# Pooled branch of a two-layer encoder: its projection made with tokens on partitions, its moving sums moved among the query and key pieces, its products moved to the second block of keys

## The chip, the cores and the metric

One core of one Trainium2 chip. The metric is the time of the device for one launch, in microseconds (us); the kernel takes some 859 of them. A core has five engines with a queue each, worked through in order: TensorE (PE in the profile, its weight loads PEld), VectorE (DVE), ScalarE (ACT), GpSimd (POOL) and SyncE (SP), which here issues most of the DMAs. Operands lie in SBUF, with 128 partitions; products are summed in PSUM.

## The reference, cut to what matters

256 tokens of width 1024, two layers. In each layer the normalised tokens are multiplied by `w_in`, whose columns are cut into the pooled branch's input `u` (1024 columns), queries, keys and values (1536 each) and two gates. What the change touches is the pooled branch: a centred mean over 2, 4, 8 or 16 tokens, minus the token, then one product per group of channels:

```python
ug = u.reshape(B, S, POOL_GROUPS, POOL_GROUP_DIM)          # 4 groups of 256 channels
pooled = jnp.stack([_centred_mean(ug[:, :, gi], w) for gi, w in enumerate((2, 4, 8, 16))], axis=2) - ug
pool_out = jnp.einsum('bsgc,gcd->bsgd', pooled, w_pool).reshape(B, S, POOL_WIDTH) * pool_scale
...
merged = jax.nn.sigmoid(g_pool) * (pool_out @ w_a) + jax.nn.sigmoid(g_attn) * (attn_out @ w_b)
return merged @ w_o
```

All of it is float32; the attention branch (three groups of four heads with a local bias) and the gated MLP with a convolution over three tokens follow beside and behind it.

## The kernel before, in words

**Products in three passes.** TensorE multiplies in fp32r. To keep the accuracy of float32, both operands are cut into a high and a low part, and three products are made: high by high, high by low, low by high. For the weights this is done as they come: SP loads a megabyte (`raw`), ACT casts half of it to the high part (`wh`, L214), DVE subtracts that to get the low part (`wl`, L216). Such a half (128 by 1024) is a *piece*, and the cast and subtraction are its *split*. `Weights` keeps the pieces in the order of use; five split pieces and three raw loads can be in SBUF at once, and `W.get()` splits as far ahead as its `look` (3, in the middle of a layer 4) and the five buffers allow. The buffer of a piece is free when PE has used it up, so in steady state the split of a piece waits for the use of the one five places earlier, and its load for the split of one six places earlier.

**Two shapes of product.** `proj` gives *channels on partitions*: the weights are the stationary operand, 128 columns at a time, and the tokens stream, 512 wide (both parts against `wh`) and 256 wide (the high part against `wl`): eight of each for 128 channels. `by_tokens` gives *tokens on partitions*: the tokens are stationary, and 512 columns of weights stream; a piece is used by 12 matmuls of 512 columns, and four pieces make 512 columns of the result for all 256 tokens, in two PSUM tiles.

**Crossing.** What is needed with channels on partitions, but was made with tokens there, goes through `cross`: two 32 by 32 block transposes of DVE out of PSUM, one write to DRAM issued by SP, and four reads back issued by POOL, each waiting for the write.

**A layer's first half, in PE's order.** Values; the pooled input (`proj`, eight times 128 channels, L577); then six groups of four pieces, made by `by_tokens` and crossed: queries and keys of block 0, of block 1, of block 2; then `w_a` on the pooled output, the gates, `w_b`, `w_o`. Values and pooled input are put in order by a scheduler. From the first block of queries to the first of the last gates the order of PE, ACT and DVE is that of the source: a dictionary `steps` says which work is recorded behind which piece (numbered 0 to 43, block 0's queries being 0 to 3), and `by_tokens` calls `step` behind each.

**The pooled branch.** For each window `w`, from 16 down to 2: two `proj` results are added up out of PSUM into `u` (with 8 tokens of zeros at each side, L613 and L614), the sums are made by doubling (L1004: one addition for window 2, four for window 16), the edges corrected (L1012, L1016), the mean minus the token made (L1018), and cut into parts (ACT L1025, DVE L1026) in `pl2`. All of that is done by the scheduler among the splits. The products with `w_pool` (`pool_out`, 16 matmuls, L577) stand one window at a time ahead of the pieces 4 to 7, the keys of block 0; from each of their two results DVE and ACT make the parts in `po2` (L1042 to L1047).

**Behind it.** `parts` cuts the crossed queries and keys of block 0 into high and low (`highs`, in the memory that held half of `pl2`), behind pieces 11 and 15. Scores of the heads begin behind piece 24, `w_a` reads `po2` from piece 24 on.

Of the kernel before, what the change touches and what calls it, by code (L numbers as in the profile page):

```python
# [17 lines left out]
P = 128  # L18
# [236 lines left out]
def encoder(ctx, tc, x, w_in, w_pool, pool_scale, w_a, w_b, w_o, norm1, norm2, w_up, conv_w,  # L255
# [45 lines left out]
    for l in range(DEPTH):  # L301
        for g in range(NG):
            c0 = C_V + g * 512
            slots = (("m2", 0, 2), ("m2", 1, 2), ("ybig",), ("at2",)) if g == 0 else ()
            for j in range(2):
                tag = "k1" if l == 0 and g == 1 and j == 0 else None
                W.use(rows(w_in[l], j * 512, 4, c0, 512, tag), slots[2 * j : 2 * j + 2])
        if l == 0:
            W.n_scaled = len(W.pieces)
        for c in range(3, -1, -1):  # L310
            W.use(cols(w_in[l], c * 256))
        for n, pairs in enumerate(BLOCKS):
            for base in (C_Q, C_K):
                pool = ([], [])
                if n == 0 and base == C_K:
                    pool = W.add(
                        w_pool[l].rearrange("g (k p) c -> p (g k) c", p=P), (8, 256),
                        [((lambda t, j=j: t[:, 4 * j : 4 * j + 4, :]), (4, 256)) for j in range(2)],
                    )
                    pool = (pool[:1], pool[1:])  # L320
                for j in range(2):
                    W.use(pool[j] + pairs_of_heads(l, j * 512, base, pairs))
        for w, c0 in ((w_a[l], 0), (w_in[l], C_GP)):
            for c in (c0, c0 + 512):
                W.use(rows(w, 0, 4, c, 512) + rows(w, 512, 4, c, 512))
        for c in (0, 512):
            W.use(rows(w_in[l], 0, 4, C_GA + c, 512) + rows(w_in[l], 512, 4, C_GA + c, 512))
            W.use(rows(w_b[l], 0, 4, c, 512))
        for c in range(4):
            W.use(rows(w_o[l], c * 256))  # L330
        first_up.append((len(W.pieces), len(W.loads)))
        slots = (("v1",), ("ybig",), ("at2",))
        for j in range(2):
            tag = None if j else "k1"
            W.use(rows(w_up[l], j * 512, 4, 0, 512, tag), slots[2 * j : 2 * j + 2])
        for j in range(2):
            W.use(rows(w_up[l], j * 512, 4, DFF, 512))
        halves_done = {}
        for kind, n in PLAN:
            if kind in "AG":  # L340
                j = halves_done.get((kind, n), 0)
                halves_done[kind, n] = j + 1
                W.use(rows(w_up[l], j * 512, 4, (kind == "G") * DFF + n * 512, 512))
            elif kind == "P":
                a = cols(w_up[l], n * P)
                if n >= 4 * NQ:
                    g = cols(w_up[l], DFF + n * P)
                    a = [a[0], g[0], a[1], g[1]]
                W.use(a)
            elif kind == "D":  # L350
                W.use(rows(w_down[l], n * P))
        n_down = sum(2 for kind, _ in PLAN if kind == "D")
        for f in range(n_down, NF, 2):
            W.use(rows(w_down[l], f * P))
# [386 lines left out]
    def cross(rows, y, z, name, after=None):  # L741
# [12 lines left out]
        for q in range(4):  # L754
# [2 lines left out]
                in_=d[:, q].rearrange("(a i) x -> i a x", i=32),  # L757
            )

    def two_parts(tag, name):  # L760


        return big.tile([P, KD, 2, 2, P], F32R, tag=tag, name=name)
# [174 lines left out]
    for l in range(DEPTH):  # L938
# [46 lines left out]
            big.tile([P, KD // 2, 2, 2, P], F32R, tag=tag, name="pl2") for tag in ("ybig", "xn")  # L985
        ]
        pooled = {}
        for gi in range(3, -1, -1):
            w = WINDOWS[gi]
            u = sm.tile([P, 2, S + 2 * PAD], F32, tag="u", name="u")  # L990
            nc.vector.memset(u[:, :, 0:PAD], 0.0)
            nc.vector.memset(u[:, :, PAD + S :], 0.0)
            for j in range(2):
                if l == 0 and (gi, j) == (1, 0):

                    with tc.issue_after(W.last_load.ins):
                        next(bias)
                add_up(in_order(u[:, j, PAD : PAD + S]), [halves(a) for a in proj(x2, 1 + (l > 0))])
            cur, n = u, S + 2 * PAD
            sh = 1  # L1000
            while sh < w:
                nxt = sm.tile([P, 2, S + 2 * PAD], F32, tag="us", name="us")
                n -= sh
                nc.vector.tensor_add(  # L1004
                    out=nxt[:, :, 0:n], in0=cur[:, :, 0:n], in1=cur[:, :, sh : sh + n]
                )
                cur = nxt
                sh *= 2
            hw = w // 2
            o = PAD - hw  # L1010
            e = edge[:, gi, 0:hw].unsqueeze(1).to_broadcast([P, 2, hw])
            nc.vector.tensor_mul(out=cur[:, :, o : o + hw], in0=cur[:, :, o : o + hw], in1=e)  # L1012
            if hw > 1:
                e = edge[:, gi, hw : w - 1].unsqueeze(1).to_broadcast([P, 2, hw - 1])
                r = slice(o + S - hw + 1, o + S)
                nc.vector.tensor_mul(out=cur[:, :, r], in0=cur[:, :, r], in1=e)  # L1016
            pd = sm.tile([P, 2, S], F32, tag="us", name="pd")
            nc.vector.scalar_tensor_tensor(  # L1018
                out=pd, in0=cur[:, :, o : o + S], scalar=1.0 / w, in1=u[:, :, PAD : PAD + S],
                op0=ALU.mult, op1=ALU.subtract,  # L1020
            )
            both = pl2[gi // 2][:, gi % 2 * 2 : gi % 2 * 2 + 2]
            ph, pl = both[:, :, 0], both[:, :, 1]
            pd = pd.rearrange("p k (m t) -> p k t m", t=2)
            nc.scalar.copy(out=ph, in_=pd)  # L1025
            nc.vector.tensor_sub(out=pl, in0=pd, in1=ph.bitcast(F32))  # L1026
            pooled[gi] = both
        def pool_out(po2):
            for j in range(2):
                i, (wh, wl) = W.get()  # L1030
                for gg in range(2):
                    for oc in range(2):
                        ps = acc.tile([P, 2, S], F32, tag="acc", name="pool_ps")
                        cc = slice(oc * P, (oc + 1) * P)
                        two_sums(
                            pooled[2 * j + gg], 2,
                            (ps, lambda k: wh[:, 2 * gg + k, cc], lambda k: wl[:, 2 * gg + k, cc]),
                        )
                        c = 4 * j + 2 * gg + oc
                        sc = hps[:, l, c : c + 1]  # L1040
                        po = sm.tile([P, 2, P], F32, tag="u", name="po")
                        nc.scalar.mul(out=po, in_=halves(ps[:, 1]), mul=sc)  # L1042
                        nc.vector.scalar_tensor_tensor(
                            out=po, in0=halves(ps[:, 0]), scalar=sc, in1=po, op0=ALU.mult, op1=ALU.add
                        )
                        nc.scalar.copy(out=po2[:, c, 0], in_=po)
                        nc.vector.tensor_sub(out=po2[:, c, 1], in0=po, in1=po2[:, c, 0].bitcast(F32))  # L1047
                    if gg:
                        W.free(i)
                    yield  # L1050

        q = big.tile([P, 2, 4, 2, P], F32, tag="q1", name="q")
        kk = big.tile([P, 2, 2 * 4, 4, 32], F32, tag="k1", name="k")
        probs, turned, ptiles = {}, {}, {}

# [73 lines left out]
        def parts(which):  # L1131

            hi = (qh, kh)[which]
            for half in range(2):
                a = kk[:, 1 - which, :, 2 * half : 2 * half + 2].rearrange("p a c j -> p c a j")
                h_, l_ = (
                    b.rearrange("p c t (a j) -> p c (t a) j", j=32)
                    for b in (hi[:, 2 * half : 2 * half + 2], lows[half][:, which])
# [3 lines left out]

        def bring(half):

            a = tmp[:, 0].rearrange("p (a c j) -> p c a j", a=8, c=4)
            nc.scalar.copy(out=q[:, half].rearrange("p c t (a j) -> p c (t a) j", j=32), in_=a)

# [2 lines left out]
        def keep_pa(n):  # L1150
# [4 lines left out]


        steps = {
            11: ((parts, 0),),
            15: ((parts, 1),),
            19: ((bring, 0),),  # L1160
            24: ((scores, 0), (start_turn, 0)),
            26: ((scores, 1), (start_turn, 1)),
# [20 lines left out]
        in_order_of_source = ExitStack()  # L1183
        in_order_of_source.enter_context(tc.manual_schedule(engines={PE, ACT, DVE}))
        W.look = W.LOOK + 1
        tmp = big.tile([P, 2, 1024], F32, tag="at2", name="qk_rows")
        po2 = None
        for n in range(6):
            block, which = divmod(n, 2)
            if n == 1:  # L1190
                po2 = two_parts("m2", "po2")
            ps = by_tokens(x2, 4, then=step, ahead=pool_out(po2) if n == 1 else None)
            y = tmp[:, 1].rearrange("p (t q c j) -> p t q c j", t=2, q=4, c=4)
            if n in (2, 4):
                z = tmp[:, 0].rearrange("p (a c j) -> p a c j", a=8, c=4)
            else:

                z = kk[:, (1, 0, None, 0, None, 1)[n]]
            cross(ps, y, z, "crossing")
            if n == 1:  # L1200

                highs = big.tile([P, 2, HPG, 2, P], F32R, tag="xn", name="highs")
                qh, kh = highs[:, 0], highs[:, 1]
# [97 lines left out]
        def to_z(ps, z, after):  # L1301
            y = big.tile([P, 2, 4, 4, 32], F32, tag="v0", name="crossing")
            cross(ps, y, z, "crossing", after)

        def of_chunk(z, i):
            return z[:, :, i].rearrange("p (t a) j -> p t a j", t=2)

        def by_halves(z):
            ps = by_tokens(x2, 4, end=2)
# [128 lines left out]
```

## Time and profile before

| | us |
|---|---|
| median of three runs | 859.02 (858.85 to 859.89) |
| profiled execution, its own time | 857.63 |
| its span, first to last instruction | 855.8 |
| granted clock of TensorE, mean | 0.997 |
| PE, PEld, DVE, ACT, POOL busy | 847.2, 710.9, 664.3, 490.5, 125.5 |
| DMA | 243 GB/s mean, 207.76 MB |

The times of instructions below come from the profiled execution; 1.8 us of its time lie outside its span. A matmul row's length contains the way through the array, so that the lengths overlap: 512 columns last 0.39 us in a row, but the next begins 0.227 us after. What PE's work takes is therefore read from the chain of work that ended last, in order of time, where every piece runs to the start of the next.

### The profile page before, as it was taken

To read this page: it belongs to the slowest core of one execution; us is meant where nothing else is said; L and a number is where in the kernel's file an instruction comes from. 1 tells how busy PE (TensorE), PEld (TensorE's weight loads), DVE (VectorE), ACT (ScalarE), POOL (GpSimd) and SP (SyncE) were. 2 spreads that over 40 slices of the span, in tenths; PEclk is the share of its full clock that TensorE was granted. 3 is DMA by queue.
4 is the path that set the end of the run, shared out by engine and by line. 5 is a ranking of instruction groups with operands and counts; after the bars stand their busy time and mean duration, and the time that the engine had idled before them with its cause. 6 is when DMAs were issued, how large, how long until landed. Compare 5 with 4: busy or idle time off the path is not lost.

```text
span 855.8 us, 11329 instructions
## 1 busy us (share of the span) xinstructions
PE 847.2 (99%) x4023; PEld 710.9 (83%) x4023; DVE 664.3 (78%) x1002; ACT 490.5 (57%) x759; POOL 125.5 (15%) x258
## 2 busy tenths in 40 slices
PE   9999999999999999999999999999999999999996
PEld 7888888888888888888888888888888888888885
DVE  7998867877767877989855977687676768887894
ACT  6756543555545566767645555455464556666682
POOL 1801123120011221220000011222100022121201
PEclk9999999999999999999999999999999999999998
DMA  9686898994749988886736578989856499798831
GB/s 327 211 258 209 255 312 259 288 314 161 245 182 296 265 274 261 272 281 220 245 100 207 183 249 270 297 261 300 274 191 253 153 283 300 250 289 273 258 136 50
DMA packets 119937, 207.76 MB, mean 243 GB/s; under 512 B 7544, under 2 KB 53312, under 8 KB 119880
## 3 DMA queue, kind: packets, MB, share of 16 engines
q1 hardware_dynamic: 112040, 185.79, 65.8%
q0 software_dynamic: 7680, 20.98, 9.2%
q8 instruction: 31, 0.51, 0.2%
q10 hardware_dynamic: 160, 0.27, 0.1%
q14 instruction: 26, 0.21, 0.1%
HBM read 182.87 MB, written 24.14 MB: 242 GB/s over the span
## 4 chain that ended last, share of the span: by engine, by line
PE 96%; DVE 2%; DMA 1%; ACT 0%; issue 0%; POOLq 0%; SPq 0%; POOL 0%; DVEq 0%; ACTq 0%
PE t_ps L701 56%; PE proj_ps L577 8%; PE v_ps L701 6%; PE res_ps L619 6%; PE res_ps L621 6%; PE res_ps L620 5%; PE v_ps L930 3%; PE v_ps L837 1%; PE pool_ps L577 1%; DMA raw<-in_w_in_dram 1%; DVE wl L216 1%; PE o_ps L1123 1%; PE s_ps L1070 1%; PE s_ps L1064 1%; PE o_ps L1119 1%; PE xt_ps L513 1%
## 5 line engine op out<-in xcount | busy, mean ns | idle before, releaser
L216 DVE TENSOR_TENSOR wl<-raw,wh 128x1024 fp32r<-128x1024 f32 x274 | 331.2, 1219 | 101.1 <-ACT wh L214 96.6
L701 PE MATMUL t_ps<-wh,x 128*128 128x512 f32 x1216 | 381.1, 390 | 0.0
L214 ACT CAST wh<-raw 128x1024 fp32r<-128x1024 f32 x274 | 285.9, 1051 | 157.4 <-PE t_ps L701 113.7
L701 PEld LDWEIGHTS t_ps<-wh,x 128*128 128x128 f32 x1216 | 228.3, 188 | 47.2
L701 PE MATMUL t_ps<-wl,x 128*128 128x512 f32 x608 | 236.6, 389 | 0.0
L701 PEld LDWEIGHTS t_ps<-wl,x 128*128 128x128 f32 x608 | 114.2, 188 | 23.7
L619 PE MATMUL res_ps<-wh,actq 128*128 128x512 f32 (+1 forms) x184 | 70.2, 381 | 0.1
L620 PE MATMUL res_ps<-wl,actq 128*128 128x512 f32 (+1 forms) x184 | 69.9, 380 | 0.0
L621 PE MATMUL res_ps<-wh,actk 128*128 128x512 f32 (+1 forms) x184 | 69.8, 380 | 0.0
L577 PE MATMUL proj_ps<-x,wh 128*128 128x512 f32 x192 | 45.7, 390 | 0.0
L755 POOL DMA_DIRECT2D k<-crossing x32 | 18.8, 594 | 175.0 <-DVE po L1047 106.9
L577 PEld LDWEIGHTS proj_ps<-x,wh 128*128 128x128 f32 x192 | 35.5, 188 | 7.0
L701 PE MATMUL t_ps<-wh,po 128*128 128x512 f32 x128 | 40.8, 393 | 0.0
L619 PEld LDWEIGHTS res_ps<-wh,actq 128*128 128x128 f32 x184 | 34.6, 188 | 7.4 <-ACT actq L1372 0.9
L621 PEld LDWEIGHTS res_ps<-wh,actk 128*128 128x128 f32 x184 | 34.6, 188 | 6.9 <-DVE actk L1373 0.4
L620 PEld LDWEIGHTS res_ps<-wl,actq 128*128 128x128 f32 x184 | 34.6, 188 | 6.6
L755 POOL DMA_DIRECT2D zga<-crossing x32 | 18.7, 590 | 104.7 <-DMA crossing<-crossing 60.1
L1356 ACT ACTIVATE y<-y 128x256 f32<-128x256 f32 x44 | 18.3, 416 | 21.3 <-DVE y L1353 20.8
L1086 ACT ACTIVATE p<-s,nm 128x512 f32<-128x512 f32 x16 | 11.6, 725 | 32.9 <-DVE nm L1083 29.6
L486 POOL TENSOR_SCALAR ss<-ss 128x1 f32<-128x1 f32 x8 | 2.0, 255 | 193.6 <-ACT junk L479 193.6
L1338 ACT ACTIVATE y<-a,prm 128x256 f32<-128x256 f32 x44 | 26.1, 598 | 6.8 <-DVE y L1357 5.9
L755 POOL DMA_DIRECT2D zg<-crossing x32 | 18.5, 584 | 76.2 <-DMA crossing<-crossing 27.4
(206 smaller groups left out, 1237.3 us busy)
## 6 DMA issues: line engine op xcount, KB each, us to landing
raw<-in_w_up_dram SPq DMA_DIRECT2D x44, 1024.0 KB, 6.6
raw<-in_w_in_dram SPq DMA_DIRECT2D x34, 1024.0 KB, 6.8
raw<-in_w_in_dram SPq DMA_DIRECT2D x50, 512.0 KB, 4.7
raw<-in_w_down_dram SPq DMA_DIRECT2D x22, 1024.0 KB, 5.9
crossing<-crossing SPq DMA_DIRECT2D x20, 512.0 KB
raw<-in_w_a_dram SPq DMA_DIRECT2D x8, 1024.0 KB, 8.7
raw<-in_w_o_dram SPq DMA_DIRECT2D x8, 1024.0 KB, 6.9
crossing<-qk_rows SPq DMA_DIRECT2D x12, 512.0 KB
```

What stands on the lines that cost most here:

```text
L214: inst = nc.scalar.copy(out=h, in_=src)
L216: inst = nc.vector.tensor_sub(out=l, in0=src, in1=h.bitcast(F32))
L577: nc.tensor.matmul(out, w(k), x, start=(steps is first and k == 0), stop=(steps is last and k == nk - 1), skip_group_check=turns["rest"],)
L619: nc.tensor.matmul(ps, ah, wh, start=first, stop=False, skip_group_check=on)
L620: nc.tensor.matmul(ps, ah, wl, start=False, stop=False, skip_group_check=on)
L621: nc.tensor.matmul(ps, al, wh, start=False, stop=last, skip_group_check=on)
L701: nc.tensor.matmul(ps, x2[:, 2 * n + j, part, t, :], w[:, j, :], start=(n + m == 0), stop=(n == last and m == 5),)
L755: nc.gpsimd.dma_start(out=z[32 * q : 32 * q + 32].rearrange("p a c j -> p a (c j)"), in_=d[:, q].rearrange("(a i) x -> i a x", i=32),)
L930: nc.tensor.matmul(ps[t], a[:, k, t, :], w[:, j, :], start=(k + m == 0), stop=(k == KD - 1 and m == 2),)
L1086: nc.scalar.activation(p, s, AF.Exp, bias=nm[:, 0:1], accum_out=z)
L1338: nc.scalar.activation(y, a, AF.Identity, bias=b, scale=w1)
L1356: nc.scalar.activation(y2, y2, AF.Tanh, scale=c)
```

## The change

- The pooled input is made by `by_tokens` in two groups of 512 columns (eight pieces), and crossed into `zu`; the loads of its weights take 512 columns and half of the rows instead of 256 columns and all rows. `u` is then copied by ACT out of `zu`.
- The sums are a generator, `pool_window`, over the windows 2, 4, 8, 16 in this order, with 18 places to stop; `steps` runs two of them behind each of pieces 4 to 6 and 8 to 12, one behind 7 and 13.
- `w_pool` and `pool_out` stand in the second block of keys: the products are ahead of pieces 12 to 15.
- `parts` for block 0's queries and keys is behind pieces 16 and 17; the keys of block 0 are crossed into `zu`'s first half, and `q` takes that memory afterwards (behind piece 19). The rows being crossed lie in `tmp`, which exists earlier.
- The results of `pool_out` use another small buffer (`p`, three of them).

```diff
-        for c in range(3, -1, -1):
-            W.use(cols(w_in[l], c * 256))
+        for c in (0, 512):
+            for j in range(2):
+                W.use(rows(w_in[l], j * 512, 4, c, 512))
         for n, pairs in enumerate(BLOCKS):
             for base in (C_Q, C_K):
                 pool = ([], [])
-                if n == 0 and base == C_K:
+                if n == 1 and base == C_K:
                     pool = W.add(
...
-        for gi in range(3, -1, -1):
+        zu = big.tile([P, 2, 8, 4, 32], F32, tag="q1", name="zu")
+        tmp = big.tile([P, 2, 1024], F32, tag="at2", name="qk_rows")
+
+        def rows_of_tmp(n):
+            return tmp[:, n].rearrange("p (t q c j) -> p t q c j", t=2, q=4, c=4)
+
+        for n in range(2):
+            ps = by_tokens(x2, 4)
+            if l + n == 0:
+
+                with tc.issue_after(W.last_load.ins):
+                    next(bias)
+            cross(ps, rows_of_tmp(1 - n), zu[:, n], "crossing", W.last[1])
+
+        def pool_window(gi):
             w = WINDOWS[gi]
             u = sm.tile([P, 2, S + 2 * PAD], F32, tag="u", name="u")
...
             for j in range(2):
-                if l == 0 and (gi, j) == (1, 0):
-
-                    with tc.issue_after(W.last_load.ins):
-                        next(bias)
-                add_up(in_order(u[:, j, PAD : PAD + S]), [halves(a) for a in proj(x2, 1 + (l > 0))])
+                c = 2 * gi + j
+                nc.scalar.copy(
+                    out=u[:, j, PAD : PAD + S].rearrange("p (a j t) -> p t a j", t=2, j=32),
+                    in_=of_chunk(zu[:, c // 4], c % 4),
+                )
             cur, n = u, S + 2 * PAD
             sh = 1
             while sh < w:
...
                 sh *= 2
+                yield
             hw = w // 2
...
                 op0=ALU.mult, op1=ALU.subtract,
             )
+            yield
             both = pl2[gi // 2][:, gi % 2 * 2 : gi % 2 * 2 + 2]
...
             pooled[gi] = both
+            yield
+
+        pool_windows = (None for gi in range(4) for _ in pool_window(gi))
+
+        def pool(n):
+            for _ in range(n):
+                next(pool_windows)
...
-                        po = sm.tile([P, 2, P], F32, tag="u", name="po")
+                        po = sm.tile([P, 2, P], F32, tag="p", bufs=3, name="po")
...
         steps = {
-            11: ((parts, 0),),
-            15: ((parts, 1),),
+
+            **{n: ((pool, 2),) for n in (4, 5, 6)},
+            7: ((pool, 1),),
+            **{n: ((pool, 2),) for n in range(8, 13)},
+            13: ((pool, 1),),
+            16: ((parts, 0),),
+            17: ((parts, 1),),
             19: ((bring, 0),),
...
-            if n == 1:
+            if n == 3:
                 po2 = two_parts("m2", "po2")
-            ps = by_tokens(x2, 4, then=step, ahead=pool_out(po2) if n == 1 else None)
+            ps = by_tokens(x2, 4, then=step, ahead=pool_out(po2) if n == 3 else None)
```

More of the change, by code (lines that the diff above doesn't have):

```diff
@@ L758, in cross, with of_chunk @@
             )
+    def of_chunk(z, i):
+        return z[:, :, i].rearrange("p (t a) j -> p t a j", t=2)
     def two_parts(tag, name):
@@ L1050, in pool_out @@
                     yield
-        q = big.tile([P, 2, 4, 2, P], F32, tag="q1", name="q")
+        q = None
         kk = big.tile([P, 2, 2 * 4, 4, 32], F32, tag="k1", name="k")
@@ L1134, in parts @@
             for half in range(2):
-                a = kk[:, 1 - which, :, 2 * half : 2 * half + 2].rearrange("p a c j -> p c a j")
+                a = (kk[:, 1], zu[:, 0])[which][:, :, 2 * half : 2 * half + 2]
+                a = a.rearrange("p a c j -> p c a j")
                 h_, l_ = (
@@ L1143, in bring @@
         def bring(half):
+            nonlocal q
+            if half == 0:
+                q = big.tile([P, 2, 4, 2, P], F32, tag="q1", name="q")
             a = tmp[:, 0].rearrange("p (a c j) -> p c a j", a=8, c=4)
@@ L1185, in encoder @@
         W.look = W.LOOK + 1
-        tmp = big.tile([P, 2, 1024], F32, tag="at2", name="qk_rows")
         po2 = None
@@ L1189, in encoder @@
             block, which = divmod(n, 2)
-            if n == 1:
+            if n == 3:
                 po2 = two_parts("m2", "po2")
-            ps = by_tokens(x2, 4, then=step, ahead=pool_out(po2) if n == 1 else None)
-            y = tmp[:, 1].rearrange("p (t q c j) -> p t q c j", t=2, q=4, c=4)
+            ps = by_tokens(x2, 4, then=step, ahead=pool_out(po2) if n == 3 else None)
+            y = rows_of_tmp(1)
             if n in (2, 4):
@@ L1196, in encoder @@
             else:
-                z = kk[:, (1, 0, None, 0, None, 1)[n]]
+                z = zu[:, 0] if n == 1 else kk[:, (1, None, None, 0, None, 1)[n]]
             cross(ps, y, z, "crossing")
-            if n == 1:
+            if n == 3:
                 highs = big.tile([P, 2, HPG, 2, P], F32R, tag="xn", name="highs")
@@ L1303, in to_z @@
             cross(ps, y, z, "crossing", after)
-        def of_chunk(z, i):
-            return z[:, :, i].rearrange("p (t a) j -> p t a j", t=2)
         def by_halves(z):
```

## The prediction

> **What bounds the kernel now.** I read the page's busy shares first, then the chain that ended last (its shares, then its pieces in order of time), then windows over the stages that the change touches, and last the timelines of TensorE (PE), VectorE (DVE) and ScalarE (ACT) inside one stage. First two parts of the page:
>
> ```profile
> span 855.8 us, 11329 instructions
> ...
> PE 847.2 (99%) x4023; PEld 710.9 (83%) x4023; DVE 664.3 (78%) x1002; ACT 490.5 (57%) x759; POOL 125.5 (15%) x258
> ...
> PE 96%; DVE 2%; DMA 1%; ACT 0%; issue 0%; POOLq 0%; SPq 0%; POOL 0%; DVEq 0%; ACTq 0%
> ```
>
> PE is the bound everywhere, so a change gains only what it takes out of PE's queue and loses whatever makes PE wait. The chain in order of time (start, length, what) in the changed stages:
>
> ```profile
> 41.39 22.27 PE proj_ps L577 x128
> 63.66 10.88 PE t_ps L701 x48
> 74.54 1.39 PE pool_ps L577 x8
> 75.93 2.73 PE t_ps L701 x12
> ...
> 86.92 1.40 PE pool_ps L577 x8
> ...
> 462.58 22.23 PE proj_ps L577 x128
> ```
>
> The pieces join without a hole: PE does not wait there in either layer. The windows (length, then busy time and count of PE, weight loads, DVE, ACT and POOL, then clock, DMA share, GB/s) say how near the other engines are:
>
> ```profile
> 41.23:63.50 22.27, 22.27 (x130) 19.68 (x128) 20.07 (x35) 12.14 (x18) 3.35 (x10) 1.00 0.86 263
> 63.50:74.37 10.87, 10.87 (x49) 9.01 (x48) 10.07 (x17) 5.84 (x7) 0.00 (x0) 1.00 0.59 182
> 74.37:90.90 16.53, 16.53 (x82) 13.93 (x81) 12.04 (x21) 9.84 (x19) 2.55 (x4) 1.00 0.82 275
> 462.42:484.65 22.23, 22.23 (x130) 19.69 (x129) 19.64 (x35) 12.37 (x18) 0.00 (x0) 1.00 0.66 211
> ```
>
> DVE is over 90% busy in the first two of them, where the moving sums lie now, and has about 4.5 us free in the third. The clock is full (1.00).
>
> **Part 1: the projection by tokens.** It replaces 128 matmuls per layer, half 512 wide, half 256 wide, by 96 matmuls 512 wide, the form of the rows of 48 that take 10.88 us. Two such groups are 21.76 us, against 22.27 and 22.23: PE gains 0.51 + 0.47 = 0.98 us. The gain lies in the narrow ones: 64 wide at 10.88/48 = 0.227 us are 14.51 us, which leaves 7.76 us for 64 narrow, 0.121 us each, against 0.113 for half a wide one.
> The Trainium skill ("TensorE: Matmul & The Clock Gate", Back-to-back issue gap) puts the spacing at N/2.4 + 2.5 ns, an estimate of 109 ns at 256 columns and 216 ns at 512. By that page the gain would be 64 times 2.5 ns, 0.16 us per layer and 0.32 in all; the row of this trace (0.227 for 512 columns) disagrees and decides.
>
> Removed from the other engines are eight PSUM copies of ACT and eight DVE additions per layer; added are two pairs of DVE transposes, eight ACT copies out of SBUF, two SP writes and eight POOL issues. In the projection stage that unloads DVE (about 20 us of 22 before), and nothing on PE is behind it. The copies on ACT are 256 wide; the nearest row, below, is 0.39 us from PSUM, and ACT has half its time free: nothing on PE's path.
>
> The crossing to the token-to-channel layout has this path, from a timeline of SP, POOL and ACT:
>
> ```profile
> 44.20 0.39 ACT L613 COPY u<-proj_ps 128x256 f32<-128x256 f32 x1
> 75.48 0.37 SPq L750 DMA_DIRECT2D crossing<-qk_rows  x1
> 80.22 2.55 POOL L755 DMA_DIRECT2D k<-crossing  x4 [35.64 <-DVE po L1047]
> ```
>
> 4.74 us from the write's issue to the reads' issue, 2.55 us of issuing, and as an estimate another 4.74 for the reads: 12 us. The first result's reader comes behind piece 4, nine pieces of 2.73 us (24.5 us) after its last matmul; the second's behind piece 8, also nine pieces after its own. Both have twice what they need. On SP the write stands ahead of the half load for pieces 4 and 5 and of the five bias loads of layer 0, and holds them some 2 us, until the transposes; those pieces are used eight to ten pieces later. On POOL only other crossings are behind the eight issues. Cost taken: nothing; bound 0 to 0.5 us per layer.
>
> **Part 2: the sums behind pieces 4 to 13.** They are 18 steps in DVE's queue, between the splits (ACT casts wh, DVE subtracts wl; one each per piece). A piece lasts 2.73 us on PE. The rows that price DVE:
>
> ```profile
> 50.62 0.70 DVE L1004 TENSOR_TENSOR us<-us 128x530 f32<-128x530 f32 x1
> 51.24 1.22 DVE L216 TENSOR_TENSOR wl<-raw,wh 128x1024 fp32r<-128x1024 f32 x1
> 52.37 0.69 DVE L1004 TENSOR_TENSOR us<-us 128x514 f32<-128x514 f32 x1
> ...
> 53.34 0.17 DVE L1012 TENSOR_TENSOR us<-us,edge 128x16 f32<-128x16 f32 x1
> 53.42 0.17 DVE L1016 TENSOR_TENSOR us<-us,edge 128x14 f32<-128x14 f32 x1
> 53.63 0.69 DVE L1018 SCALAR_TENSOR_TENSOR pd<-us,u 128x512 f32<-128x512 f32 x1
> 54.23 1.22 DVE L216 TENSOR_TENSOR wl<-raw,wh 128x1024 fp32r<-128x1024 f32 x1
> 55.37 0.69 DVE L1026 TENSOR_TENSOR pl<-pd,pl 128x512 fp32r<-128x512 f32 x1
> ```
>
> From start to start: split 1.14, sum 0.62 (0.74, its whole length and 0.04, when the next one needs its result: so long the scaling waits behind the edge at 53.42), scaling 0.60, remainder 0.61 as an estimate from the scaling, of the same width. Two steps are about 1.3 us, with the split 2.45: under 2.73, so from piece to piece DVE keeps up, and each split waits for its buffer as it does now. Only a crossing's transposes (1.3 us, once in four pieces) push it over.
>
> **Part 3: the products in the second block of keys.** Now they stand ahead of pieces 4 to 7, with every sum long done; in the changed order of the built program they stand ahead of pieces 12 to 15, and the last remainder (window 16) comes behind piece 13, for a product ahead of piece 15. Between are, in DVE's order: split of the second pooled weight; two sums; the transposes of query block 2; split 14; two results of window 2; the last sum, edges and scaling; two results of window 4; splits 15 and 16; the remainder. The rows for these, from the same stage now:
>
> ```profile
> 74.38 0.61 PE L577 MATMUL pool_ps<-pl,wh 128*128 128x512 f32 x2
> 74.62 1.05 ACT L214 CAST wh<-raw 128x1024 fp32r<-128x1024 f32 x1 [1.65 <-PE t_ps L701]
> ...
> 74.14 1.31 DVE L748 STREAM_TRANSPOSE qk_rows<-t_ps 128x512 f32<-128x512 f32 x2
> 75.70 1.23 DVE L216 TENSOR_TENSOR wl<-raw,wh 128x1024 fp32r<-128x1024 f32 x1 [0.25 <-ACT wh L214]
> 76.85 0.48 DVE L1043 SCALAR_TENSOR_TENSOR po<-pool_ps,hps,po 128x256 f32<-128x256 f32 x1
> ...
> 79.19 0.43 DVE L1047 TENSOR_TENSOR po<-po,po 128x256 fp32r<-128x256 f32 x1 [0.47 <-ACT po L1046]
> 79.96 0.48 DVE L1043 SCALAR_TENSOR_TENSOR po<-pool_ps,hps,po 128x256 f32<-128x256 f32 x1 [0.35 <-ACT po L1042]
> ...
> 83.20 3.50 DVE L216 TENSOR_TENSOR wl<-raw,wh 128x1024 fp32r<-128x1024 f32 x3 [0.53 <-ACT wh L214]
> ```
>
> Clock zero is PE's end of piece 10, which frees the buffer for the second pooled weight. A piece ends at 74.38 and its split starts at 75.70, so DVE starts at 1.32. Then: split (75.70 to 76.85) to 2.47; two sums (0.74 + 0.62) to 3.83; transposes, 1.31 less the 0.08 by which a next instruction overlaps, to 5.06; split 14 to 6.21; the results of window 2, held by trips to ACT (76.85 to 79.19 + 0.38), 2.72, to 8.93; sum, edges and scaling 0.73 + 0.08 + 0.21 + 0.60 to 10.55; results of window 4 and the wait for ACT's cast (79.96 to 83.20) 3.24, to 13.79; two splits 2.28 to 16.07; the remainder in full 0.69 and, an estimate from the gap behind the edge, 0.05 to wake PE: 16.81. PE arrives after piece 11 (2.73) and three times product and piece (74.54 to 86.92: 12.38) at 15.11. **PE waits 1.7 us** in each layer, at the last window's first product. It takes products in order, and the pieces behind (15 on) can't go round it. What hides the sum now is that its chain ends 20 us before its use; here two pieces of cover are too few.
>
> The price between bounds: 1.2 if the two sums and the results' trips go faster, 2.4 if the second pooled weight's split starts late behind the sums of window 8 (by my rows it starts with 0.1 us to spare). Behind it: split 18 is done after split 17, the results of windows 8 and 16 and itself (1.15 + 2.72 + 3.24 + 1.15 = 8.3 us behind the remainder), PE wants it after one product and three pieces (9.6); then the transposes of key block 2 come about 6 us later than they could, and what they feed is needed nine pieces later. No second wait.
> Moved too: the pooled weight's load and its 16 products, same time on PE; the high/low parts of queries and keys, from behind pieces 11 and 15 to 16 and 17, seven pieces before the scores. Cost nothing.
>
> **The sum.** Against the profiled execution (857.63 us, of it 855.8 span): minus 0.98, plus 2 x 1.70: 860.05. The three runs have their median 1.39 higher: **861.4**.
>
> **Rivals.** (a) *The cover holds*: DVE gets the last remainder out before PE needs it; the place is the product ahead of piece 15, the point 15.1 us after piece 10. For it: DVE's windows show slack of 4.5 us in 16.5 where products stand now. Against: the sum above misses by 1.7, and its waits are those that the same work has in the trace. Then only part 1 is left: 858.0. If half the deficit is made good, 859.7.
> (b) *The stage of pieces 4 to 12 falls behind*: a crossing that lands late in layer 0 (DMA share 0.86 there) holds ACT's copy and all casts behind it. PE has four split pieces, 11 us, in hand. Each microsecond over that costs one: 862.8 to 866. Against: 24.5 us for a 12 us path.
> (c) *The stall lets the clock drop*: PE is now never idle in these stages, and every window there shows 1.00, so no row tells what 1.7 us does. If a product and a piece (4.13 us) ran at half speed behind each stall, 2 x 4.13 more: 869.7. The Trainium skill ("TensorE: Matmul & The Clock Gate", the section on the HAM clock gate) has the clock fall only after an idle window of about 3.4 us; by that page 1.7 us leave it, and (c) would need a stall twice as long.
> That the change does not do what it says is out: the built order shows it.
>
> **How the numbers follow.** 0.2%, 1.7 us, is about what a measurement of this kernel can tell from no change: 857.3 to 860.7. Forecast 0.70, with stalls of 1.2 to 2.4: 860.4 to 862.8, most of it (0.62) above 860.7. Cover holds 0.15, half of it 0.06: same. (b) 0.04 and (c) 0.02: slower. A gain beyond part 1 that no row shows: 0.03, faster. So slower 0.68, same 0.29, faster 0.03. The range takes in the forecast and (a), which together with the half case leave under 0.1 outside: 857.9 to 863.0; the forecast's own is 860.4 to 862.8.
>
> **What would show it.** In the changed profile the two projection stages should be 21.76 us of t_ps without a hole; the chain should have one DVE link in each layer (remainder, line L1046 of the changed kernel) before the pooled product of the last window, and the waits of PE should name it with 1.2 to 2.4 us each. Wrong if PE is seamless there, if the wait is at window 8's product or at a split (a wider backlog), if an ACT copy waits for a crossing, or if a window behind the stall shows a clock under 1.00.

## The result, and the profile after

The changed kernel takes 862.89 us (median of six runs, 862.27 to 866.0), the one before 858.93 in six runs beside it (857.61 to 859.89): slower by a ratio of 1.0054 (95% interval 1.0036 to 1.0072). Three more rounds later gave 863.37 against 858.51, ratio 1.0061 (1.0048 to 1.0074). The forecast was 861.4: the sign is right, the time is above the forecast's own range (860.4 to 862.8) and at the upper end of the whole one (863.0), which the later median passes. Single runs of either kernel differ by 2 us and more, so the terms below are read from traces.

The profiled execution took 862.41 us, 860.6 of it span. The parts of its page that stood in the prediction:

```profile
span 860.6 us, 11236 instructions
...
PE 848.0 (99%) x3959; PEld 708.6 (82%) x3959; DVE 664.5 (77%) x994; ACT 489.5 (57%) x759; POOL 133.3 (15%) x274
...
PE 84%; DVE 9%; DMA 3%; issue 1%; ACT 1%; SPq 1%; POOLq 0%; DVEq 0%; POOL 0%; ACTq 0%
```

PE has fewer instructions and the same busy share; what is new is the chain: 9% of it are DVE's, which had 2%. What PE waited for behind the kernel's first microseconds is one line of the view of waits (us in total, times, longest); the place comes from the chain in order of time below it:

```profile
PE pool_ps L578 <- DVE pl L1046: 3.8, 2, 1.9
```

```profile
41.28 8.17 PE t_ps L702 x36
...
105.82 1.05 ACT wh L214
106.96 1.08 issue
108.03 1.22 DVE wl L216
...
110.00 1.64 PE pool_ps L578 x8
111.64 27.21 PE t_ps L702 x120
...
464.22 32.66 PE t_ps L702 x144
```

The chain leaves PE at 49 us and comes back to it at 110.00, at the pooled product of the last window, which waited for the remainder (L1046). The same windows as before, and one more behind the wait in layer 1 (length, busy time and count of PE, weight loads, DVE, ACT, POOL, then clock, DMA share, GB/s):

```profile
41.12:62.88 21.76, 21.76 (x98) 18.02 (x96) 12.38 (x12) 9.01 (x9) 4.09 (x7) 1.00 0.84 259
62.88:73.76 10.88, 10.88 (x50) 9.01 (x48) 6.03 (x7) 4.12 (x4) 0.91 (x2) 1.00 1.07 340
73.76:95.52 21.76, 21.76 (x98) 18.02 (x96) 20.76 (x38) 12.81 (x19) 3.87 (x8) 1.00 0.97 288
95.52:107.90 12.38, 12.38 (x61) 10.25 (x59) 9.81 (x19) 6.16 (x12) 3.97 (x8) 1.00 0.77 244
107.90:110.00 2.10, 0.16 (x1) 0.03 (x1) 2.10 (x4) 1.78 (x3) 0.46 (x1) 1.00 0.79 202
532.80:536.20 3.40, 3.38 (x10) 2.86 (x11) 2.46 (x5) 1.42 (x4) 0.00 (x0) 0.52 1.05 359
```

First row: the pooled input is 21.76 us where it was 22.27, as worked out. First to third: DVE, which was 90% busy from the projection on, is now busy for only 12.38 of 21.76 us in the projection and 6.03 of 10.88 in query block 0, and is then 95% busy over pieces 4 to 11. Fifth: PE waits 2.10 us, DVE not at all. Last: behind the wait of layer 1 the clock is 0.52, in a stage where the kernel before had 1.00 throughout.

PE's own rows give the waits (start, length, what, idle time and releaser):

```profile
107.67 0.39 PE L702 MATMUL t_ps<-wh,x 128*128 128x512 f32 x1
110.00 0.70 PE L578 MATMUL pool_ps<-pl,wh 128*128 128x512 f32 x2 [1.94 <-DVE pl L1046]
```

```profile
530.61 0.39 PE L702 MATMUL t_ps<-wh,x 128*128 128x512 f32 x1
532.82 1.06 PE L578 MATMUL pool_ps<-pl,wh 128*128 128x512 f32 x2 [1.82 <-DVE pl L1046]
```

From start to start less the usual 0.23, that is 2.10 and 1.98 us. The two matmuls behind last 0.70 us together in layer 0 and 1.06 in layer 1: that is the clock. The trace's record has half clock for one stretch of 3.41 us from 532.96 on, which costs 1.7. The account: -0.51 - 0.47 + 2.10 + 1.98 + 1.7 = +4.8, and the span went from 855.8 to 860.6. The medians moved by 3.96 and 4.86.

### The profile page after: what moved, and what is told of

It is laid out like the page before. It is cut to its first block, busy times and chain, and to the rows that moved or that the text cites. A ratio compares the mean times of both kernels' runs of the same rounds, so it can differ in the third digit from the quotient of the medians.

```text
span 860.6 us, 11236 instructions
## 1 busy us (share of the span) xinstructions
PE 848.0 (99%) x3959; PEld 708.6 (82%) x3959; DVE 664.5 (77%) x994; ACT 489.5 (57%) x759; POOL 133.3 (15%) x274
## 4 chain that ended last, share of the span: by engine, by line
PE 84%; DVE 9%; DMA 3%; issue 1%; ACT 1%; SPq 1%; POOLq 0%; DVEq 0%; POOL 0%; ACTq 0%
PE t_ps L702 51%; PE v_ps L702 6%; PE res_ps L620 6%; PE res_ps L622 5%; PE res_ps L621 5%; DVE wl L216 4%; DMA raw<-in_w_in_dram 3%; PE v_ps L934 3%; PE proj_ps L578 2%; PE v_ps L841 1%; DVE us L1022 1%; PE o_ps L1151 1%; PE s_ps L1098 1%; DVE qk_rows L749 1%; PE s_ps L1092 1%
## 5 line engine op out<-in xcount | busy, mean ns | idle before, releaser
L702 PE MATMUL t_ps<-wh,x 128*128 128x512 f32 x1344 | 421.2, 390 | 0.0
L702 PEld LDWEIGHTS t_ps<-wh,x 128*128 128x128 f32 x1344 | 252.7, 188 | 52.7
L702 PE MATMUL t_ps<-wl,x 128*128 128x512 f32 x672 | 261.7, 389 | 0.0
L702 PEld LDWEIGHTS t_ps<-wl,x 128*128 128x128 f32 x672 | 126.4, 188 | 25.9
L756 POOL DMA_DIRECT2D zu<-crossing x24 | 14.2, 596 | 103.6 <-PE t_ps L702 63.0
L702 PEld LDWEIGHTS t_ps<-wh,po 128*128 128x128 f32 x128 | 24.0, 188 | 4.9
L756 POOL DMA_DIRECT2D turned_p<-turning x32 | 18.6, 590 | 55.9 <-DMA turning<-turning 30.8
```

The costliest lines, as they stand in the source:

```text
L702: nc.tensor.matmul(ps, x2[:, 2 * n + j, part, t, :], w[:, j, :], start=(n + m == 0), stop=(n == last and m == 5),)
L756: nc.gpsimd.dma_start(out=z[32 * q : 32 * q + 32].rearrange("p a c j -> p a (c j)"), in_=d[:, q].rearrange("(a i) x -> i a x", i=32),)
```

## The experiments

Theory A: the last remainder stands too late in DVE's queue. Theory B: DVE has too much to do there, wherever it stands. Theory C: a wait of this length lets PE's clock fall.

**remainder_12.** The remainder moved ahead of two results and two splits, same work.

```diff
-            **{n: ((pool, 2),) for n in range(8, 13)},
-            13: ((pool, 1),),
+            **{n: ((pool, 2),) for n in range(8, 12)},
+            12: ((pool, 3),),
```

> The changed kernel with one step moved: the last remainder (window 16) is recorded behind piece 12, together with its scaling, and no longer behind piece 13. Same work on every engine. Theory A (the place in DVE's queue): the remainder no longer stands behind the results of window 4 and the splits 15 and 16, 5.5 us of DVE; it ends some 3 us before the last window's product, split 15 comes about 1.4 us later and just in time, no wait of PE over 0.3 us in either layer, full clock throughout: 858.0, that is 1.0 below the kernel before. Theory B (DVE has too much to do in pieces 4 to 13, wherever it stands): the work is the same, so a wait of 1.5 to 2 us per layer shows up at split 15 or at the product instead: 861 to 863.

860.96 us against 858.23 (1.0033, 1.0020 to 1.0047). Both theories have a part. The wait at the product is gone; in both layers another of 1.03 us, from start to start less the usual, stands at piece 18's low part instead. PE's line in the view of waits, and its row in layer 0:

```profile
PE t_ps L702 <- DVE wl L216: 1.5, 2, 0.8
```

```profile
120.63 0.50 PE L702 MATMUL t_ps<-wl,x 128*128 128x512 f32 x1 [0.76 <-DVE wl L216]
```

As this trace has it, place cost about 1.0 us of each 2.0 and load the other 1.0. The changed kernel shows nothing at split 18, presumably because its first wait gave DVE the time. The two waits less the 0.98 of part 1 make 1.1 us, and the medians differ by 2.7: the waits do not account for all of it (see the end of the next section).

**steps_3_to_11.** All steps earlier and denser.

```diff
+            **{n: ((pool, 2),) for n in range(3, 12)},
```

> The changed kernel with all 18 steps one to two pieces earlier: two behind each of pieces 3 to 11. Theory A: the last remainder ends before the first pooled product, no wait of PE, full clock: 858.0. The sums of window 8 come behind piece 6 and need the second crossing 19 us after its matmuls, about when it landed in the changed kernel's layer 0; if that lands late, ACT holds the casts behind it, but four split pieces are in hand. Theory B: the work per piece from 3 to 11 is as dense as before, so splits come late: 860 to 863.

862.04 (1.0058, 1.0030 to 1.0086): a miss for A alone. In the trace layer 0 waits 0.59 us and layer 1 0.36 inside the third pooled product (window 8's, at 106.72 and 531.98 us), for the result of an earlier product, and 1.00 and 1.01 at split 18; smaller ones follow at the scores and their products. PE's line for the third product:

```profile
PE pool_ps L578 <- DVE po L1071: 0.6, 2, 0.4
```

DVE is further behind, not ahead. That the density of the steps does it, two behind every piece and some with a trip to ACT between, is argued here, not varied by itself.

**wait_layer_0, wait_layer_1.** The changed steps in one layer, those of steps_3_to_11 in the other.

> The changed kernel's steps in layer 0, the earlier steps (behind 3 to 11) in layer 1. Theory A: layer 0 waits 2.1 us as before, layer 1 not: 858.0 + 2.1 = 860.1. If the clock's fall behind the wait of layer 1 belongs to that wait (half clock for 3.4 us, 1.7 us lost), then there is none here; if a wait of 2 us brings it down by chance in either layer, some runs show 861.8.

> The earlier steps (behind 3 to 11) in layer 0, the changed kernel's steps in layer 1. Theory A: layer 1 waits 2.0 us as before, layer 0 not: 860.0 without a fall of the clock, 861.7 with half clock for 3.4 us behind the wait. If the fall comes by chance, runs of both times are seen.

864.19 (1.0065, 1.0040 to 1.0090) and 863.41 (1.0063, 1.0036 to 1.0090): both are above what was expected, and neither separates the layers by its time, because the earlier steps bring waits of their own. For the waits and the clock their traces serve: 2.09 us in layer 0 of the first, 1.99 in layer 1 of the second. The windows behind them:

```profile
111.20:114.70 3.50, 3.49 (x11) 2.92 (x12) 2.56 (x5) 1.52 (x4) 0.00 (x0) 0.52 1.07 329
```

```profile
532.70:536.20 3.50, 3.46 (x17) 3.01 (x18) 2.55 (x5) 1.49 (x4) 0.00 (x0) 1.00 1.04 354
```

0.52 behind the one in layer 0, 1.00 behind the one in layer 1, the reverse of the changed kernel: the fall belongs to no layer.

**steps_2_to_12.** The steps over more pieces.

```diff
+            **{n: ((pool, 2),) for n in (2, 3, 4)},
+            5: ((pool, 1),),
+            **{n: ((pool, 2),) for n in range(7, 12)},
+            12: ((pool, 1),),
```

> The changed kernel with the sums spread further: windows 2 and 4 behind pieces 2 to 5, windows 8 and 16 behind pieces 7 to 12, the last remainder alone behind piece 12. The two earlier runs with the steps moved show that place alone is not all: DVE has more to do between pieces 3 and 18 than PE leaves it time for, some 1.0 us per layer that came out at split 18. Theory AB (place and load): two more pieces of DVE's free time (2 x 1.6 us) take up that 1.0 us: no wait of PE over 0.3 us, 1.0 below the kernel before. If the wait at split 18 has another cause (its place behind eight results, whatever came before), 1.0 us per layer stays: 1.1 above.

858.02 against 858.48 (1.0001, 0.9991 to 1.0012). In the trace theory A with B holds: of the 4 us of waits 0.35 us are left, at split 18 in layer 0; in layer 1 PE does not wait. The time does not show the gain of 1.0 that was expected: its interval takes in no change and ends short of 1.0 below (0.9988).

**proj_2_to_12.** The same with the old projection, its loads again in columns of 256.

```diff
-        for n in range(2):
-            ps = by_tokens(x2, 4)
-            ...
-            cross(ps, rows_of_tmp(1 - n), zu[:, n], "crossing", W.last[1])
+        for c in range(8):
+            ...
+            sums = [a.rearrange("p (t a j) -> p t a j", t=2, a=4) for a in proj(x2, 1 + (l > 0))]
+            add_up(of_chunk(zu[:, c // 4], c % 4), sums)
```

> The kernel steps_2_to_12 with part 1 undone: the pooled input is made by proj with channels on partitions, as before, and its sums are added up out of PSUM into the place that the crossing filled; no crossing of it. Everything behind is the same. If part 1 is worth 0.98 us on PE, the stage is 22.25 us again and this run is 0.5 us per layer behind steps_2_to_12, about equal to the kernel before where PE does not wait. By equal cost of equal columns the two would differ by 0.3 us or less.

858.9 against 858.48 (1.0006, 0.9996 to 1.0015), 0.9 behind steps_2_to_12. Its chain has the stage at the old length in one piece (22.23 in layer 1), and no wait of PE in these stages:

```profile
41.16 22.27 PE proj_ps L577 x128
```

So part 1 is worth its 0.98 us, and not the small gain of equal cost for equal columns. The medians lie that way (0.9 apart), but the two intervals overlap and would not carry it alone.

**light_sums.** Three of the four additions of window 16 are left out in each layer, so its pooled values are not the reference's; DVE has 2.0 us less to do.

```diff
             while sh < w:
+                if w == 16 and sh > 1:
+                    sh *= 2
+                    yield
+                    continue
```

> The changed kernel with its steps where they are, but three of the four additions of window 16 left out in each layer (the pooled values of that window are not the reference's): 2.0 us less for DVE between the split of the second pooled weight and the last remainder. By the sum of the prediction the wait for the remainder (2.1 and 2.0 us) falls by those 2.0 us to 0.1 or nothing, and with it the 1.0 us of load that showed at split 18: 0.8 to 1.0 below the kernel before. If the wait comes from something that is not DVE's work (the second pooled weight's load, a buffer of PSUM), it stays near 2 us: 3 to 5 above.

857.7 against 858.48 (0.9988, 0.9979 to 0.9997). The chain runs through the stages with 0.10 us more than usual at the last product:

```profile
41.12 54.40 PE t_ps L702 x240
95.53 1.39 PE pool_ps L578 x8
...
105.17 2.73 PE t_ps L702 x12
107.90 1.49 PE pool_ps L578 x8
```

A wait that shrinks from 2.1 to 0.1 us when 2.0 us of DVE's work is left out is a wait for that work.

**remainder_14.** The remainder one piece later.

```diff
-            13: ((pool, 1),),
+            14: ((pool, 1),),
```

> The changed kernel with the last remainder recorded one piece later, behind piece 14, right ahead of the product that needs it. It then stands behind split 17 and the results of window 8 too (1.1 + 2.7 us): the wait grows from 2.0 to 5.8 us per layer. For the clock: a wait of 2 us brought it down where it lay inside one of its windows of 3.41 us and left it up where it lay across two. A wait of 5.8 us holds a whole window wherever it begins, so both layers should show 0.5 for at least 3.4 us behind it, 1.7 us each: 2 x 5.8 + 2 x 1.7 - 1.0 = 14 above the kernel before. If the fall is not tied to the wait, 10.6 above.

873.27 against 858.48, 14.8 more, near the 14 that was expected with a fall in both layers and not the 10.6 without. The waits are 6.02 and 5.96 us, and behind both the clock is down:

```profile
PE pool_ps L578 <- DVE pl L1046: 11.7, 2, 5.9
```

```profile
115.10:118.40 3.30, 3.28 (x10) 2.82 (x11) 0.58 (x2) 1.01 (x3) 0.00 (x0) 0.52 0.50 175
543.20:548.50 5.30, 5.26 (x15) 4.39 (x16) 1.77 (x4) 2.44 (x5) 0.00 (x0) 0.52 0.41 144
```

The half clock is recorded for 6.83 us in each layer, two windows and not one; part of it lies in the wait itself. That a wait of 5.8 us holds a whole window wherever it begins does not follow: for that it would have to last 6.83. Both waits here held one.

**bias_later.** From steps_2_to_12, with the sums of windows 8 and 16 a piece earlier (6 to 11) and layer 0's bias table stored and loaded ahead of the first keys instead of in the pooled input's stage.

```diff
-            if l + n == 0:
-
-                with tc.issue_after(W.last_load.ins):
-                    next(bias)
...
+            if l == 0 and n == 1:
+
+                with tc.issue_after(W.last_load.ins):
+                    next(bias)
```

> steps_2_to_12 with its last wait in view (0.35 us at split 18 of layer 0, none in layer 1): in layer 0 the second crossing of the pooled input landed 19 us after its matmuls, while the bias table's five loads were in the same queue. Here the bias table is stored and loaded behind the first block of queries, and the sums of windows 8 and 16 begin one piece earlier (pieces 6 to 11; windows 2 and 4 stay behind 2 to 5). If that crossing lands in some 12 us as in layer 1, PE waits nowhere in these stages and the kernel is 1.0 below the one before. If the loads only move the crowd, ACT waits for a later crossing and 0.3 to 1 us stays in layer 0.

859.18 against 858.51 (1.0012, 1.0002 to 1.0021): a miss in layer 0 (waits of 0.44 and 0.98 us), right in layer 1 (none). The loads moved the crowd. ACT's timeline in layer 0:

```profile
92.47 2.00 ACT L214 CAST wh<-raw 128x1024 fp32r<-128x1024 f32 x2 [4.73 <-DMA raw<-in_w_in_dram]
```

Casts stand still for 4.73 us on a weight load that is now behind the bias loads in SP's queue.

**spread_bias_later.** The steps of steps_2_to_12, the bias table another group of pieces later, behind the keys of block 0 (`n == 2`).

> steps_2_to_12 (windows 2 and 4 behind pieces 2 to 5, windows 8 and 16 behind 7 to 12) with the bias table stored and loaded behind the first block's keys. In the trace of steps_2_to_12 DVE stood still from 65 to 70.6 us in layer 0, waiting for loads that came behind the bias loads; that put it 3 to 4 us behind and left 0.35 us of wait at split 18. Without those loads in front, DVE starts on time, PE waits nowhere in these stages in either layer: 1.0 below the kernel before. If something waits for the bias loads where they are now, 0.3 to 1 us stay.

857.85 against 858.44 (0.9994, 0.9983 to 1.0004); the interval takes in no change as well as the expected 1.0 below. Its profiled execution has a span of 854.6, 1.2 below that of the kernel before; 0.3 of these lie ahead of the pooled input, where both kernels compute the same. PE waits nowhere in these stages, in either layer. DVE's row in steps_2_to_12 shows what went away (idle time in brackets):

```profile
70.57 2.36 DVE L216 TENSOR_TENSOR wl<-raw,wh 128x1024 fp32r<-128x1024 f32 x2 [4.96 <-ACT wh L214]
```

**changed_again.** The changed kernel itself.

> The changed kernel itself, for another trace and more times. The waits are fixed by the queue: 2.0 to 2.1 us in each layer again. The clock behind them depends on where a window of 3.41 us begins: with both waits across two windows 3.1 above the kernel before, with one of them inside a window 4.8, with both 6.5; in the trace, a wait that lies inside one window has 0.5 behind it and one across two has not.

863.37 against 858.51, 4.86 more: as was expected for one fall. The waits are 2.03 and 1.98 us; the windows behind them:

```profile
110.95:114.40 3.45, 3.45 (x17) 2.96 (x18) 2.51 (x5) 1.49 (x4) 0.00 (x0) 1.00 1.05 330
533.67:537.60 3.93, 3.93 (x12) 3.29 (x13) 2.99 (x6) 1.55 (x4) 0.00 (x0) 0.57 1.06 360
```

## Why the prediction was right and wrong

- **What bounds, part 1.** Right: 21.76 us per layer, 0.98 in all, shown by the stage's window and by proj_2_to_12. The 0.32 that the prediction gives for equal cost is a slip: 128 matmuls become 96 in each layer, so 32 fewer at its 2.5 ns are 0.08 us, and 0.16 in all.
- **The place of the wait.** Right: the only waits of PE on another engine in these stages are at the last window's first product, for the remainder, once in each layer.
- **Its price.** Too small: 1.70 forecast, 2.10 and 1.98 measured. The step that failed is the first term, the start of the second pooled weight's split. DVE's timeline:

```profile
94.52 1.22 DVE L216 TENSOR_TENSOR wl<-raw,wh 128x1024 fp32r<-128x1024 f32 x1
95.65 1.46 DVE L1022 TENSOR_TENSOR us<-us 128x538 f32<-128x538 f32 x2
97.03 1.31 DVE L749 STREAM_TRANSPOSE qk_rows<-t_ps 128x512 f32<-128x512 f32 x2
...
106.89 2.36 DVE L216 TENSOR_TENSOR wl<-raw,wh 128x1024 fp32r<-128x1024 f32 x2 [0.52 <-ACT wh L214]
109.17 0.69 DVE L1046 TENSOR_TENSOR pl<-pd,pl 128x512 fp32r<-128x512 f32 x1
```

  PE should have come to the product at 107.90, so piece 10 ended 15.11 us before, at 92.79; the split starts at 94.52, 1.73 behind it and not 1.32 (1.64 in layer 1). From there to PE's start at 110.00 are 15.48 us; the sum had 15.49 (16.81 - 1.32). Everything behind that first term held. The term was 0.3 to 0.4 too small because "from piece to piece DVE keeps up" was wrong. From the split at 75.12 to the one at 94.52, seven pieces on, are 19.40 us, in which DVE's timeline marks no wait for another engine; seven pieces last 19.04 on PE. The prediction's 2.45 us for a split and two steps left out the small instructions: at the head of each window two fills of the margins of `u` (L1009, L1010; 0.2 us to the start of the sum, four times in this stretch), and the edges (L1031, L1035; 0.20 to 0.28 us, three times). They make 1.6 us; without them, as an estimate from these rows, the stretch would be 17.8 and DVE in time. The head of the first window:

```profile
75.12 1.23 DVE L216 TENSOR_TENSOR wl<-raw,wh 128x1024 fp32r<-128x1024 f32 x1 [0.35 <-ACT wh L214]
76.30 0.07 DVE L1009 MEMSET u<- 128x16 f32 x1
76.33 0.07 DVE L1010 MEMSET u<- 128x16 f32 x1
76.50 0.72 DVE L1022 TENSOR_TENSOR us<-u 128x542 f32<-128x542 f32 x1
77.26 0.16 DVE L1031 TENSOR_TENSOR us<-us,edge 128x2 f32<-128x2 f32 x1
77.46 0.69 DVE L1037 SCALAR_TENSOR_TENSOR pd<-us,u 128x512 f32<-128x512 f32 x1
```

  The prediction had a late split as its upper bound (2.4).
- **The clock.** Wrong, and the larger part. Rival (c), taken at 0.02, came in one of the two layers in both traces of the changed kernel: 1.7 us each time, not the 4.1 assumed per layer. The step that failed is the clock's term, put at nothing: the waits of 2 us could bring it down. Whether one of 1.7 us would have is not shown. A window under 1.00 behind the stall was among the prediction's own signs of being wrong. The Trainium skill ("TensorE: Matmul & The Clock Gate", the section on the HAM clock gate) asks for an idle window of about 3.4 us; the windows measured here are 3.41 us long, but a wait of 1.98 us brought the clock down, so PE need not be idle for a whole one.
- **Rival (a), the cover holds.** Did not come; light_sums shows by how much it failed.
- **Rival (b), the crossing.** It cost next to nothing, but the path's 12 us were too short. The crossings landed 13 to 15 us after their last matmuls, and the second of layer 0 only after 19 (at 82.0 us): beside the bias loads, with a DMA share of 0.84 and 1.07 in the first two windows, its reads were issued 10 us behind its last matmul:

```profile
72.86 2.30 POOL L756 DMA_DIRECT2D zu<-crossing x4 [12.12 <-DMA crossing<-qk_rows]
```

  That is still inside the 24.5 us before its reader. The weight loads behind the bias loads are in the chain of layer 0 until 73.96, but ACT's cast behind them begins 33.86 us before PE is due at the last product, and the same cast of layer 1 33.94 us before: 0.08 us of difference.
- **"No second wait."** Right for this kernel, but perhaps only since the first wait gave DVE the time: without that wait, remainder_12 showed 1.0 us at split 18.

Part of the spread lies at the start, ahead of every edit. In seven of the thirteen traces the clock is full from 3.7 to 4.6 us on, and the pooled input begins at 40.9 to 41.2 us. In four it is full only from 8.5 to 9.8 us on, and in two (remainder_12, steps_2_to_12) half again from 7.0 to 10.4; there the pooled input begins at 42.1 to 42.9. So 1 to 2 us between two profiled executions need not come from an edit. Not settled: how the runs without a trace divide, and what else is in their spread.

## What to carry to other kernels

A kernel that never lets its bounding engine wait gains only by what leaves that engine's queue; moving work out of its shadow needs the same care as adding work. Before moving steps of a second engine, add up its whole load, with the small fills and edges, between the first and the last place that must be met, with its idle time in the stage that the data's longer way leaves empty: here the crossing emptied DVE in one stage and filled the next, and only spreading the steps over more pieces, with the queue of loads in mind, kept PE busy. A short wait costs more than its length when it lets the clock fall (here 1.7 us more).

## What the runs showed of the hardware that was not expected

The clock's windows. The changed kernel's half clock lasted 3.413 us, and its trace then has full clock for 320.85 us, 94 times as long, up to the next change; in remainder_14 the full clock between the two falls lasted 423.25 us, 124 times as long. So the clock changes at the ends of windows of 3.413 us, as these records have it. Counted from the ends of the recorded stretches, the six waits of 2 us in the traces begin at 0.91, 1.17, 1.29, 1.39, 1.40 and 1.60 us into a window. The first three, which end before the window does by 0.14 us or more, had half clock in the next window and the last three, which end at most 0.03 us before its end or behind it, had not. Waits of 1.0 to 1.2 us (in remainder_12, steps_3_to_11, wait_layer_0, wait_layer_1 and bias_later) never had, though four of the eight lay inside one window. So the same wait cost 2.0 us or 3.7, by where in a window it began.

What decides is open. The idle share of the window, as counted here, does not: it was 58, 61 and 58% in the three windows with a fall behind them, and 59, 58 and 53% in the three without. If the windows ended 0.1 us ahead of the recorded change, the shares would be 58, 61 and 58 against 56, 56 and 50% and could decide; no run varies this.
